# Small-tile mixer products gathered into pinned visits between a decoder trunk's streamed products

## The chip, the core and the metric

The kernel runs on one NeuronCore of a Trainium2 chip. The metric is the device time of one execution in microseconds (us); lower is better. The engines are PE (TensorE: matmul), ACT (ScalarE), DVE (VectorE), POOL (GpSimd) and SP (SyncE, which issues most of the transfers from the chip's memory).

## What is computed

Two layers of a decoder trunk for one prompt of 256 tokens and 8 samples of 4 tokens, 288 columns in all, in 32-bit floats.

```
u = RMSNorm(x)                                  1024 wide
cols = u @ W_in                                 four mixers and four gates
o_A = conv4 -> RG-LRU, times GeLU gate          256 wide
o_B = RWKV-7 delta-rule state, 4 heads of 64
o_C = HGRN2, 4 heads, state 128 x 64
o_D = dilated sliding-window attention, 4 heads of 64, over cached keys for the samples
x += W_o( sum_n sigmoid(G_n) * (o_n @ P_n) )
x += W_down( gelu(causal_dwconv3(v @ W_gate)) * (v @ W_up) ),   v = RMSNorm(x)
then a last RMSNorm
```

The outputs are the trunk's result and every mixer's new states.

## The kernel before

Activations lie with features on the 128 partitions and the 288 tokens along the columns. A weight chunk of 128 x 1024 comes by one transfer into a buffer `w`, is split by ACT into a rounded half `h` and by DVE into the remainder `l` (`chunk`, three buffers each), and gives 24 products of 128 x 128 weights with 288 columns: for each of eight input blocks high x high, high x low and low x high (`prod`). These are the **streamed** products, 3600 in a layer: 30 chunks of projection (`proj`, numbered by `PROJ`), four gates of eight chunks (`gates`), each followed by the branch product with `in_wb`, then the output projection and the feed-forward part.

`ORDER = "pA pB pC g0 g2 pD g1 g3"` is the order of the streamed work up to the output projection: the projections of mixer A (4 chunks), B (8) and C (12), gate 0 with the branch product of A, gate 2 with that of C, the projections of D (6), gate 1 with that of B, gate 3 with that of D. In chunks of 24 products that is 4 + 8 + 12 + 10 + 10 + 6 + 10 + 10 = 70; this stretch is called the mixing stage here. A branch product cannot start before its mixer has put its result into `ys`.

The mixers are Python generators (`branch_a`, `branch_b`, two of `branch_c`, `branch_d`) that run while the program is traced. `unit` emits nine or six streamed products and then calls `mix`, which lets up to four mixers go on to their next `yield`; `GAP` sets how many calls a mixer of a kind then sits out. B starts a second generator for its samples (kind S, `samples` in `branch_b`), D one for the attention over the cached keys (kind E, `samples` in `branch_d`). So the tracing gives an order in the program text. From it the framework's scheduler makes each engine's final order with its own model of times, by readiness and by place in the text; it hands out tile buffers in that order too. PE, like the other engines, then runs its list as it stands.

The mixers' products are of two sorts. Some use the whole array (in the profile 128*128, or 96*128): transposes `tr`, group sums `exact` over the constant `blk`, and state products. Others use a smaller array tile: 64*128, 128*64, 64*64, 64*32, 128*32, 32*64 or 32*32 rows and columns, several of them side by side. `quads` of B, a recursive inverse, makes 32*32 products; `level_out` of C makes 64-column blocks for seven levels of a decay tree, at the first three with a further small product for the samples; `scores` of B and D makes 64*128 ones. PSUM has eight banks: `pm` 3 for streamed results, `xb` 2 for B, S and E, `xc` 3 for A, C, D and the norms. The tag `b` has 20 buffers, for B and, later, for the feed-forward's activations (`hparts`).

C ends with a product over `zs` that gives the samples' output, a state update, then squares, a sum over `blk` (tiles `a`), logarithm, exponential, three multiply steps and a split into `y`. E loads 16 blocks of keys (`in_kc`, `load_k`) and 16 of values (`in_vc`, `load_v`), four at a time, into the tag `c2` of ten buffers.

Of the kernel before, what the change touches and what calls it, by code (L numbers as in the profile page):

```python
# [127 lines left out]
def dkeys():  # L128
# [7 lines left out]
        "tmp": (1152, 4), "rs": (1152, 1), "a": (1280, 10), "b": (1152, 20), "kb": (2048, 10), "c2": (2688, 10), "kc": (2048, 7),  # L136
# [3 lines left out]
GAP = {"B": 2, "S": 0, "C": 1, "D": 1, "E": 3}  # L140
STEPS = 4
# [9 lines left out]
def trunk(ctx, tc, I, O):  # L151
# [25 lines left out]

    def mm(o, a, b, start=True, stop=True):
        return nc.tensor.matmul(o, a, b, start=start, stop=stop)  # L179
# [269 lines left out]
    def branch_a(l, cols, rs, ys):  # L449
# [26 lines left out]
        for i in range(2):  # L476
# [3 lines left out]
            for j in range(1, 4):  # L480
                stt(xc, e[:, j:j + w], pcol(l, "acw", 2 * j + i), xc, MUL, ADD)
            pg, pa = X("xc")[:, :w], X("xc")[:, :w]
            mm(pg, gw[:, i], xc)
            mm(pa, gw[:, 2 + i], xc)
            yield
# [35 lines left out]
    def branch_b(l, cols, rs, ys_, spawn):  # L521
# [25 lines left out]
        at, rt, bt, kt, bv, elast = [], [], [], [], [], []  # L547
# [3 lines left out]
        pre = []  # L551
        for i in range(2):
            f = slice(i * P, (i + 1) * P)

            pw, pa = X("xb")[:, :N], X("xb")[:, :N]
            first = mm(pw, lora[0:64, 0, f], wa[0:64])
            with tc.issue_after(first.ins):
                mm(pa, lora[64:128, 0, f], wa[64:128])

            kk = T("b")  # L560
            act(kk, k[i], AF.Square, scale=pcol(l, "kk", i))
            yield
            lw, ta = T("b"), T("b")
# [7 lines left out]
        for i in range(2):  # L571
            pn = X("xb")[:, :N]
            exact(pn, bones, pre[i][3], "b")
            yield
            ts(pre[i][3], pn, 1e-24, MAX, float(2 ** 20), MUL)
# [4 lines left out]
        for i in range(2):  # L580
# [6 lines left out]
            b = T("b")  # L587
            stt(b, ta, 1.0, kk, ADD, MUL)

            ep, em = T("b"), T("b")  # L590
# [26 lines left out]
            stt(rk, rk, pcol(l, "rk", i), k2, MUL, MUL)  # L617
            pb = X("xb")[:, :N]
            exact(pb, bones, rk, "b")
            yield  # L620
# [5 lines left out]
        def samples():  # L626
# [4 lines left out]
            p = X("xb")  # L631
# [5 lines left out]
            yield  # L637
# [11 lines left out]
            p = X("xb")  # L649
            for h in range(4):  # L650
                i, z = h // 2, 64 * (h % 2)
                one = ident[rows(h), rows(h)]
                mm(p[z:z + NS, i * 64:i * 64 + 64], bt[i][rows(h), sc], one)
                mm(p[z + NS:z + 64, i * 64:i * 64 + 64], kt[i][rows(h), sc], one)
            act(stk[:, :P], p[:, :P], AF.Copy)
            uv = R([P, 2, 64], "sm")
            for h in range(4):
                z = 64 * (h % 2) + NS
                G.tensor_copy(uv[z:z + NS, h // 2], vh[hr(h)])
            p = X("xb")  # L660
            for h in range(4):
                mm(p[hr(h), :NS], abT[hr(h)], Xi[hr(h)])
            yield
            act(t1, p[:, :NS], AF.Copy)
            p = X("xb")
            for h in range(4):
                mm(p[hr(h), :NS], t1[hr(h)], Y[hr(h)])
            yield
# [7 lines left out]
            for src in (at, rt):  # L676
                p = X("xb")
                for h in range(4):
                    mm(p[hr(h)], src[h // 2][rows(h), sc], s0[h // 2][rows(h)].rearrange("p b v -> p (b v)"))
                yield  # L680
# [3 lines left out]
                sar.append(t)  # L684
            p = X("xb")
            for h in range(4):
                mm(p[hr(h), :64], zs[hr(h), 0], vh[hr(h)])
            yield
            rr, u = T("sm", 64), T("sm", 64)
            tt(V, rr, p[:, :64], sar[0], ADD)  # L690

            p = X("xb")
            for h in range(4):
                mm(p[hr(h), :64], Y[hr(h)], rr[hr(h)])
            yield
            act(u, p[:, :64], AF.Copy)
            for h in range(4):
                z = 64 * (h % 2)
                G.tensor_copy(uv[z:z + NS, h // 2], u[hr(h)])
            for i in range(2):  # L700
                p = X("xb")
# [5 lines left out]
            yield  # L707

            for i in range(2):
                ue = R([P, NB, 64], "kb")  # L710
                tt(G, ue, bc(uv[:, i], 1, [P, NB, 64]), bc(C("vexp"), 2, [P, NB, 64]), MUL)
                p = X("xb")
                for z in range(2):
                    mm(p[rows(z)], stk[rows(z), i * 64:i * 64 + 64], ue[rows(z)].rearrange("p b v -> p (b v)"))
                yield
# [9 lines left out]
        def scores(a, q):  # L725

            ps_ = [X("xb"), X("xb")]
# [6 lines left out]
        ab, abo = (R([P, 8, 64], "kb") for _ in range(2))  # L734
        sab = scores(bt, at)
        yield
# [12 lines left out]
        for pair in (((0, bt, 0), (0, kt, 1)), ((0, v, 2), (1, v, 2)), ((1, bt, 0), (1, kt, 1))):  # L749
            p = X("xb")  # L750
            for n, (i, src, _) in enumerate(pair):
                for c in range(2):
                    tr(p[:, (2 * n + c) * P:(2 * n + c + 1) * P], src[i][:, c * P:(c + 1) * P])
            yield
            for n, (i, _, m) in enumerate(pair):
                tk[i][m] = T("b", 256)
                act(tk[i][m], p[:, n * TP:(n + 1) * TP], AF.Copy)
# [8 lines left out]
        def quads(a, b, to=(0, 1, 2, 3), src=(0, 1, 2, 3)):  # L766

            p = X("xb")
# [5 lines left out]
        for m in (2, 4, 8, 16):  # L774
            p = quads(ab[:, :, 0:32], X4)
            yield
            t1 = R([P, 8, 32], "kb")
            act(t1, p, AF.Copy)
            p = quads(Y4, t1)
            yield  # L780
            V.copy_predicated(X4, Mn(f"l{m}", 8), p)
            V.transpose(fl(Y4), fl(X4))

        Y, Xi = R([P, 8, 64], "kb"), R([P, 8, 64], "kb")
        G.memset(Y, 0.0)
        G.memset(Xi[0:64], 0.0)
        p = quads(ab[:, :, 32:64], X4, (1, 3), (0, 2))
        yield
# [8 lines left out]
        p, p2 = quads(t1, Y4, (0, 2), (1, 3)), quads(Y4, t1, (1,), (1,))  # L797
        yield
# [3 lines left out]

        p = blocks(abo, Xi, (0,), 1)
        yield
        t1, Z = R([P, 8, 64], "kb"), R([P, 8, 64], "kb")
        act(t1[64:128], p[64:128], AF.Copy)
        G.tensor_copy(Z[64:128], Y[64:128])
        p = blocks(t1, Y, (1,), 0)
        yield
# [3 lines left out]
        zz = [[], []]  # L813
        for a, q, mk in ((kt, at, "us"), (bt, rt, "ui"), (kt, rt, "ui")):
            pair = scores(a, q)
            yield
            for h, p in enumerate(pair):
                z = R([P, 4, P], "kb")
                G.memset(z, 0.0)
                V.copy_predicated(z, Mn(mk, 4), p)  # L820
                zz[h].append(z)
        def hc(h):
            return slice(64 * h, 64 * h + 64)
        st = None
        for c in range(2):
            s = slice(c * P, c * P + P)
            p = X("xb")
# [7 lines left out]
            yield  # L835
            rr = T("b", 256)
            act(rr, p[:, :256], AF.Copy)
            p = X("xb")
# [5 lines left out]
            yield  # L844
            u = R([P, 2, P], "b")
            act(fl(u), p[:, :256], AF.Copy)
            p = X("xb")
# [5 lines left out]
            yield  # L853
# [15 lines left out]
            p = X("xb")  # L869
            for i in range(2):  # L870
                if c:
                    mm(p[:, i * P:(i + 1) * P], st[:, i], rt[i][:, s], start=True, stop=False)
                for m in (2, 1):
                    for h in range(2):
                        o, tc_ = p[rows(h), i * P:(i + 1) * P], slice(c * P + 64 * h, c * P + 64 * h + 64)
                        mm(o, tk[i][2][:, tc_] if m == 2 else u[:, i, hc(h)], zz[h][m][:, 2 * i + c],
                           start=c == 0 and m == 2, stop=m == 1)
            yield
            for i in range(2):
                act(py[i][:, s], p[:, i * P:(i + 1) * P], AF.Copy)  # L880
# [5 lines left out]
        for i in range(2):  # L886
            p = X("xb")[:, :N]
            exact(p, cent, py[i], "b")
            yield
# [4 lines left out]
        for i in range(2):  # L894
            p = X("xb")[:, :N]
            exact(p, bones, sqs[i], "b")
            yield
# [3 lines left out]
        for i in range(2):  # L901
            sq, yc = sqs[i], py[i]
            stt(yc, yc, pcol(l, "lnw", i), sq, MUL, MUL)
            stt(yc, yc, pcol(l, "lnb", i), bv[i], ADD, ADD)
# [698 lines left out]
```

## Time and profile before

| | |
|---|---|
| median of three runs | 1210.65 us (1209.11 to 1214.6) |
| profiled execution, its own time | 1212.02 us |
| its span, first to last instruction | 1210.2 us |
| PE, DVE, ACT, POOL busy | 97%, 70%, 51%, 46% of the span |
| PE instructions | 10564 matmuls |
| mean transfer rate | 162 GB/s |
| mixing stages with small products | 54 to 346 us and 649 to 939 us |

Busy time of PE is the union of its instructions' spans, and a matmul's end is modelled; a busy PE can still run at less than its best rate. What a product costs is read from the starts of neighbouring ones. In a timeline row the first number is the start, the second how long the group took, and x the count of products in it.

### The profile page before, as it was taken

Reading aid. Unit: us, or ns where it says so; the run is one execution under the profiler, and the core shown is the slowest. Engines: PE = TensorE matmul, PEld = TensorE weight load, DVE = VectorE, ACT = ScalarE, POOL = GpSimd, SP = SyncE. Lnnn points to the kernel's source line nnn. Section 1 sums busy time; section 2 is a strip of 40 time slices with the busy share of each in tenths; the row PEclk is TensorE's granted clock in tenths of the full one; section 3 lists DMA queues with packets and bytes.
Section 4 is the critical chain, followed back from the end, with each engine's and each line's share of the span. In section 5 each row is a group of like instructions: output and inputs, shape, how many; then the busy total and the mean of one; then the engine's idle time right before and its main releaser. Section 6 shows DMA issues by size and latency. Waiting matters only on the chain.

```text
span 1210.2 us, 26415 instructions
## 1 busy us (share of the span) xinstructions
PE 1172.3 (97%) x10564; PEld 1102.2 (91%) x10564; DVE 848.4 (70%) x1385; ACT 611.3 (51%) x1042; POOL 552.8 (46%) x864
## 2 busy tenths in 40 slices
PE   7998999999999999999998999999999999999997
PEld 6987788998999999999998977899889999999996
DVE  7898856566578888865568888566655878888543
ACT  5776447445355444443367844565444554444332
POOL 3744555250345665642238337524221736665322
PEclk9999999999999999999998999999999999999999
DMA  7444145357645555454543432643775445545552
GB/s 258 132 130 141 63 152 203 112 168 277 209 133 190 161 171 168 164 176 163 171 153 124 141 106 89 214 145 115 253 250 168 150 152 171 172 158 171 167 171 77
DMA packets 64043, 196.33 MB, mean 162 GB/s; under 512 B 8417, under 2 KB 12641, under 8 KB 63921
## 3 DMA queue, kind: packets, MB, share of 16 engines
q1 hardware_dynamic: 61872, 189.56, 47.4%
q0 software_dynamic: 1328, 4.33, 1.0%
q8 instruction: 83, 1.36, 0.5%
q10 hardware_dynamic: 720, 0.76, 0.2%
q14 instruction: 40, 0.32, 0.1%
HBM read 187.08 MB, written 6.49 MB: 160 GB/s over the span
## 4 chain that ended last, share of the span: by engine, by line
PE 74%; DVE 9%; POOL 6%; ACT 4%; DMA 4%; issue 3%; DVEq 0%; SPq 0%; ACTq 0%; POOLq 0%
PE pm L179 43%; PE xc L179 24%; PE xb L179 5%; DVE c L193 2%; DVE l L193 2%; POOL b L193 1%; ACT L185 1%; DMA c<-in_vc 1%; DMA w<-in_w 1%; DVE b L196 1%; POOL a L193 1%; ACT a L185 1%; ACT h L185 1%; PE xc L182 1%; DMA kc<-in_cs 1%
## 5 line engine op out<-in xcount | busy, mean ns | idle before, releaser
L179 PE MATMUL pm<-tp,h 128*128 128x288 f32 x2880 | 608.3, 302 | 3.8 <-ACT h L185 2.3
L185 ACT ACTIVATE h<-w 128x1024 fp32r<-128x1024 f32 x299 | 316.5, 1059 | 393.8 <-issue 182.1
L179 PEld LDWEIGHTS pm<-tp,h 128*128 128x128 f32 x2880 | 471.3, 191 | 17.7 <-issue 7.3
L193 DVE TENSOR_TENSOR l<-w,h 128x1024 fp32r<-128x1024 f32 x299 | 380.6, 1273 | 118.6 <-ACT h L185 117.6
L179 PE MATMUL pm<-tp,l 128*128 128x288 f32 x1440 | 430.4, 299 | 4.5 <-DVE l L193 4.5
L179 PEld LDWEIGHTS pm<-tp,l 128*128 128x128 f32 x1440 | 274.7, 191 | 7.1 <-DVE l L193 5.0
L179 PE MATMUL xc<-tp,h 128*128 128x288 f32 x896 | 183.9, 296 | 1.6 <-ACT tp L185 0.9
L179 PEld LDWEIGHTS xc<-tp,h 128*128 128x128 f32 x896 | 144.7, 188 | 3.3 <-ACT tp L185 1.3
L179 PE MATMUL xc<-tp,l 128*128 128x288 f32 x448 | 132.3, 295 | 0.0
L193 POOL TENSOR_TENSOR tmp<-a,rs 128x256 f32<-128x256 f32 x96 | 73.5, 785 | 71.7 <-ACT a L185 71.7
L193 POOL TENSOR_TENSOR tp<-tp,th 128x288 f32<-128x288 f32 x48 | 52.3, 1111 | 109.3 <-DVE th L196 109.3
L196 DVE SCALAR_TENSOR_TENSOR a<-a,pv,a 128x304 f32<-128x304 f32 (+2 forms) x112 | 83.8, 749 | 11.2 <-ACT a L185 9.5
L179 PEld LDWEIGHTS xc<-tp,l 128*128 128x128 f32 x448 | 84.3, 188 | 0.4 <-DVE l L193 0.4
L193 POOL TENSOR_TENSOR tmp<-x 128x288 f32<-128x288 f32 x28 | 28.2, 1008 | 108.2 <-DVE x L193 107.9
L193 DVE TENSOR_TENSOR th<-pm,rs 128x288 f32<-128x288 f32 x64 | 29.1, 455 | 59.3 <-PE pm L179 59.2
L193 POOL TENSOR_TENSOR c<-c 128x512 f32<-128x512 f32 (+2 forms) x32 | 36.9, 1173 | 35.4 <-DVE kb L193 25.4
L193 DVE TENSOR_TENSOR tmp<-pm,tmp 128x288 f32<-128x288 f32 x48 | 22.0, 458 | 40.1 <-POOL tmp L193 40.1
L185 ACT ACT_TABLE_LOAD x34 | 43.6, 1283 | 0.6
L185 ACT ACTIVATE c<-c 128x256 f32<-128x256 f32 (+2 forms) x68 | 30.6, 500 | 20.9 <-POOL c L193 15.5
L185 ACT ACTIVATE a<-a 128x304 f32<-128x304 f32 (+2 forms) x76 | 33.6, 445 | 13.6 <-DVE a L196 7.8
L193 DVE TENSOR_TENSOR c<-c,c 128x256 f32<-128x256 f32 (+2 forms) x56 | 38.8, 734 | 1.7 <-ACT c L185 1.4
L179 PE MATMUL pm<-y,h 128*128 128x288 f32 x192 | 39.8, 299 | 0.0
(302 smaller groups left out, 1879.1 us busy)
## 6 DMA issues: line engine op xcount, KB each, us to landing
w<-in_wf SPq DMA_DIRECT2D x96, 512.0 KB, 3.5
w<-in_wg SPq DMA_DIRECT2D x64, 512.0 KB, 3.8
w<-in_w SPq DMA_DIRECT2D x59, 512.0 KB, 3.6
w<-in_wd SPq DMA_DIRECT2D x48, 512.0 KB, 3.5
c<-in_kc SPq DMA_DIRECT2D x32, 320.0 KB, 6.2
c<-in_vc SPq DMA_DIRECT2D x32, 320.0 KB, 5.3
w<-in_wb SPq DMA_DIRECT2D x16, 512.0 KB, 3.6
w<-in_wo SPq DMA_DIRECT2D x16, 512.0 KB, 3.5
```

Of the source, the lines that this page charges most:

```text
L179: return nc.tensor.matmul(o, a, b, start=start, stop=stop)
L182: nc.tensor.transpose(o, i, ident)
L185: S.activation(o, i, f, **kw)
L193: e.tensor_tensor(o, a, b, op)
L196: V.scalar_tensor_tensor(o, a, s, b, op0, op1)
```

## The change

- Every product is traced in a kind: streamed (`s`), of a visit (`v`), or a full-array product of a mixer (`f`). With `behind`, an ordering edge on PE, each product of a visit is tied behind the one before it, the first behind the last streamed product traced, and the next streamed product behind the visit's last. The `f` products are not tied, nor are the other streamed ones to each other.
- `mix` now runs the steps of kind `f` at each call, but those of kind `v` only once 22 or more streamed products have gone by since the last visit. As calls come after 9, 9 and 6 products, that is after 24. A step's own wait is counted in streamed products too: 9 after an `f` step, 18 before the next `v` step, and 30, 36 or 48 where the text says so. `STEPS` and `GAP` are gone.
- Where a mixer must wait for something before the streamed work can go on, `mix(True)` lets time run on without streamed products.
- Yields now stand ahead of the products instead of behind them, and steps are joined: both first-stage products of B in one step; the samples' second product of S with the first; each C level with its sample product, levels 4 and 8 as one step, 16 and 32 as one; in B's scores, `kt` against `at` and `rt` side by side in one tile `ar` (8 products of 256 columns for 16 of 128); in B's chunks, state and output products in one step; in E, key blocks 0 and 1, 2 and 3, value blocks 0 and 1, 2 and 3.
- Some small products become full-array ones: transposes of 32 columns now take 128, and C's sample transposes go with the others. B's token-major transposes become a generator of their own.
- `b` goes from 20 to 16 buffers, a new tag `ar` has two of 2304 bytes, `exact` in B takes its two halves from `yb`.

```diff
-GAP = {"B": 2, "S": 0, "C": 1, "D": 1, "E": 3}
-STEPS = 4
+VISIT = 22
...
+    kind, now, last = ["s"], [0], {"s": None, "v": None, "open": False}
+
+    def behind(ins, prev):
+        tc.add_manual_dep(ins.ins, prev.ins.name, mybir.DependencyInfo(
+            mybir.DependencyClass.NoSync, mybir.DependencyReason.DATA), reason="order on PE")
+
     def mm(o, a, b, start=True, stop=True):
-        return nc.tensor.matmul(o, a, b, start=start, stop=stop)
+        ins = nc.tensor.matmul(o, a, b, start=start, stop=stop)
+        if kind[0] == "v":
+            behind(ins, last["v"] if last["open"] else last["s"])
+            last["v"], last["open"] = ins, True
+        elif kind[0] == "s":
+            if last["open"]:
+                behind(ins, last["v"])
+                last["open"] = False
+            last["s"] = ins
+            now[0] += 1
+        return ins
...
+        for i in range(2):
+            yield "v"
+            pair = [X("xb"), X("xc")]
+            for c in range(2):
+                s = slice(c * P, c * P + P)
+                for h in range(2):
+                    mm(pair[h][:, c * TP:(c + 1) * TP], kt[i][rows(h), s], ar[i][rows(h), :, s])
...
+            level = (d, d, f"u{m}", f"s{m}" if m <= 2 else None)
+            if m in (4, 16):
+                first = level
+                continue
+            yield "v", 30
+            level_out(*([level] if m <= 2 else [first, level]))
...
                 for g in range(4):
                     mm(s1[quarter(g), 0:P], qb[:, j, 2 * g + n // 2], ks[g][:, 512:640], start=f, stop=z)
-                yield
                 if n < 2:
                     load_k(n + 2)
+                if n == 1:
+                    yield "v", 48
...
+        def steps(which):
+            for x in list(mixers):
+                if x[1] > now[0] or (x[2] == "v") != (which == "v"):
+                    continue
+                kind[0] = which
+                try:
+                    state = next(x[0])
+                except StopIteration:
+                    mixers.remove(x)
+                    continue
+                finally:
+                    kind[0] = "s"
+                gap = 0
+                if state != "wait":
+                    state, gap = state if isinstance(state, tuple) else (state, 0)
+                    gap = max(gap, 18 if state == "v" else 9)
+                x[1], x[2] = now[0] + gap, state
+
+        def mix(idle=False):
+            steps("f")
+            if idle or now[0] - visited[0] >= VISIT:
+                visited[0] = now[0]
+                steps("v")
+            if idle:
+                now[0] += 9
...
             while n not in ys:
-                mix()
+                mix(True)
```

## Rows read from the trace of the kernel before

**Rows 1.** Windows: us, busy us (count) of PE, PEld, DVE, ACT, POOL; clock; DMA share, GB/s.
```profile
54.00:346.00 292.00, 282.26 (x3031) 250.58 (x3031) 198.88 (x353) 157.07 (x318) 121.52 (x176) 0.98 0.48 161
390.00:480.00 90.00, 90.00 (x683) 90.00 (x682) 74.87 (x117) 41.47 (x59) 57.87 (x109) 1.00 0.53 169
649.00:939.00 290.00, 280.70 (x3024) 249.01 (x3022) 198.34 (x350) 155.30 (x317) 118.16 (x170) 0.98 0.49 162
100.00:155.00 55.00, 49.79 (x667) 40.39 (x666) 47.91 (x90) 25.16 (x59) 29.93 (x36) 0.97 0.25 83
```

**Rows 2.** Timeline of PE, first and last small-tile group of the first layer.
```profile
55.85 0.76 PE L179 MATMUL xb<-b,kb 64*128 64x288 f32 x4
...
319.09 1.30 PE L179 MATMUL xb<-c,c 128*32 128x128 f32 x40
```

**Rows 3.** Timeline of PE around one small-tile group of E.
```profile
309.55 0.42 PE L179 MATMUL pm<-yb,h 128*128 128x288 f32 x2
309.81 0.29 PE L179 MATMUL pm<-yb,l 128*128 128x288 f32 x1
310.03 1.30 PE L179 MATMUL xb<-c,c 128*32 128x128 f32 x40
311.26 0.53 PE L179 MATMUL pm<-yb,h 128*128 128x288 f32 x2
311.63 0.29 PE L179 MATMUL pm<-yb,l 128*128 128x288 f32 x1
```

**Rows 4.** Timeline of PE, a narrow window: the last four of those forty.
```profile
311.04 0.29 PE L179 MATMUL xb<-c,c 128*32 128x128 f32 x4
```

**Rows 5.** Timeline of PE, narrow windows: one small tile straight after another.
```profile
119.37 0.63 PE L179 MATMUL xb<-kb,b 64*32 64x512 f32 x4
...
119.82 0.61 PE L179 MATMUL xb<-kb,b 64*32 64x512 f32 x4
...
120.36 0.45 PE L179 MATMUL xc<-c,c 128*64 128x64 f32 x8
```

**Rows 6.** Waits of PE: total us, times, longest.
```profile
PE xb L179 <- ACT b L185: 6.2, 2, 3.4
...
PE pm L179 <- DVE l L193: 4.5, 3, 2.1
PE xc L179 <- DVE c L193: 4.1, 6, 1.1
```

**Rows 7.** Windows of the lowered clock in the mixing stages, first and last.
```profile
70.03:73.44 3.41, 3.41 (x16) 3.41 (x16) 3.41 (x7) 3.39 (x8) 1.61 (x3) 0.50 0.07 26
...
704.91:708.32 3.41, 3.41 (x17) 3.41 (x15) 3.41 (x9) 0.29 (x1) 2.39 (x4) 0.50 0.45 150
```

**Rows 8.** Timelines of PE, ACT and POOL: C's end and the product that needs it.
```profile
201.09 0.67 PE L179 MATMUL xc<-a,blk 128*128 128x288 f32 x3
...
201.92 0.50 ACT L185 ACTIVATE a<-xc,few 128x288 f32<-128x288 f32 x1
202.44 1.28 ACT L185 ACT_TABLE_LOAD   x1
...
211.21 0.80 POOL L193 TENSOR_TENSOR y<-a,y 128x288 fp32r<-128x288 f32 x1 [4.43 <-ACT y L185]
213.17 1.61 POOL L193 TENSOR_TENSOR y<-a,y 128x288 fp32r<-128x288 f32 x1 [1.17 <-ACT y L185]
...
231.36 0.54 PE L179 MATMUL pm<-y,h 128*128 128x288 f32 x2
```

**Rows 9.** Timeline of PE at the mixing stage's end.
```profile
346.86 0.40 PE L179 MATMUL xc<-tp,h 128*128 128x288 f32 x1 [0.45 <-ACT tp L185]
347.10 0.43 PE L179 MATMUL pm<-y,h 128*128 128x288 f32 x2
```

**Rows 10.** Transfers by line: count, KB each, median us to landing.
```profile
c<-in_kc SPq DMA_DIRECT2D x32, 320.0 KB, 6.2
```

**Rows 11.** Windows, columns as in rows 1: the stretch of E's key loads.
```profile
270.00:300.00 30.00, 30.00 (x239) 23.48 (x232) 18.71 (x41) 14.99 (x36) 1.98 (x5) 1.00 0.80 283
```

More of the change, by code (lines that the diff above doesn't have):

```diff
@@ L550, in branch_b @@
         els = R([P, 2, NB], "sm")
-        pre = []
+        pre, pwa = [], []
+        yield "v"
         for i in range(2):
             f = slice(i * P, (i + 1) * P)
[L555 to L558, printed above, removed]
+            pwa.append((X("xb")[:, :N], X("xc")[:, :N]))
+            for z, p in enumerate(pwa[i]):
+                mm(p, lora[rows(z), 0, f], wa[rows(z)])
+        for i in range(2):
+            pw, pa = pwa[i]
             kk = T("b")
             act(kk, k[i], AF.Square, scale=pcol(l, "kk", i))
-            yield
-            lw, ta = T("b"), T("b")
+            ar.append(R([P, 2, N], "ar"))
+            lw, ta = ar[i][:, 0], T("b")
             act(lw, pw, AF.Tanh, scale=0.5, bias=dcol(l, "hw0", i))
@@ L636, in samples @@
                 mm(p[hr(h), P:P + 64], v[h // 2][rows(h), sc], ident[rows(h), rows(h)])
-            yield
+            for h in range(4):
+                i, z = h // 2, 64 * (h % 2)
+                one = ident[rows(h), rows(h)]
+                mm(p2[z:z + NS, i * 64:i * 64 + 64], bt[i][rows(h), sc], one)
+                mm(p2[z + NS:z + 64, i * 64:i * 64 + 64], kt[i][rows(h), sc], one)
             abT, Y, Xi, t1 = (T("sm", NS) for _ in range(4))
@@ L648, in samples @@
             act(vh, p[:, P:192], AF.Copy)
[L649 to L655, printed above, removed]
+            act(stk[:, :P], p2[:, :P], AF.Copy)
             uv = R([P, 2, 64], "sm")
@@ L843, in branch_b @@
                     mm(p[64:128, o], Z[:, z], rr[:, o])
-            yield
             u = R([P, 2, P], "b")
             act(fl(u), p[:, :256], AF.Copy)
-            p = X("xb")
+            yield "v"
+            p, po = X("xb"), X("xc")
+            if c:
+                for i in range(2):
+                    mm(po[:, i * P:(i + 1) * P], st[:, i], rt[i][:, s], start=i == 0, stop=False)
             for i in range(2):
@@ L852, in branch_b @@
                         mm(o, tk[i][m][:, tc_], tk[i][2][:, tc_] if m else u[:, i, hc(h)], start=m == 1, stop=m == 0)
-            yield
+            for i in range(2):
+                for m in (2, 1):
+                    for h in range(2):
+                        o, tc_ = po[rows(h), i * P:(i + 1) * P], slice(c * P + 64 * h, c * P + 64 * h + 64)
+                        mm(o, tk[i][2][:, tc_] if m == 2 else u[:, i, hc(h)], zz[h][m][:, 2 * i + c],
+                           start=c == 0 and m == 2, stop=m == 1 and c <= i)
             if c == 0:
@@ L868, in branch_b @@
                 nc.sync.dma_start(O["b_wkv_p"][l], nst)
-            p = X("xb")
             for i in range(2):
[L871 to L880, printed above, removed]
+                act(py[i][:, s], po[:, i * P:(i + 1) * P], AF.Copy)
             st = nst
@@ L1400, in gates @@
             while n not in ys:
-                mix()
+                mix(True)
             y = ys[n]
@@ L1432, in trunk @@
         while mixers:
-            mix()
+            mix(True)
         mg = []
```

260 lines of the change are left out of this document (132 added, 128 removed).

## The prediction

> **What bounds the kernel now.** I read the windows first. In the feed-forward stretch PE is busy all the time and starts 683 products in 90 us [rows 1]: 0.132 us for a streamed product, and PE is the limit. The two mixing stages take 292 and 290 us with the clock at 0.98 and PE busy 96 to 97% [rows 1]. Of their 70 chunks of 24 products about 53 fall into these windows, so streamed work explains 53 x 24 x 0.132 = 168 us; some 123 us in each layer go to mixer products, to changing between array tiles, and to waits. That is where the change acts. In the part from 100 to 155 us DVE is busy 47.9 of 55 us [rows 1], so there it is nearly as full as PE.
>
> Next, the timeline of PE, for what a change of array tile costs. Between streamed products the start moves on 0.13 us at a time (309.55 for two, 309.81). The first small product starts at 310.03, 0.22 after the last streamed one: 0.09 late [rows 3]. The forty run four abreast; from 310.03 to the last four at 311.04 is nine steps of 0.112 us; the first streamed product follows after 0.22, at 311.26, so 0.11 late [rows 3, 4]. The next pair takes 0.37 to 311.63 where 0.26 is usual: 0.11 more [rows 3]. One small-tile group between streamed products, a *visit*, thus costs 0.31 us beside its own work. Straight from one small tile to another: four products of 64*32 take 0.45, the next four 0.54 until the 128*64 ones start [rows 5]: 0.09.
>
> I counted the groups in the timeline from the first to the last of the first layer [rows 2]: 65 visits, and 33 direct changes inside them; the second layer has the same numbers.
>
> Third, the waits of PE: 6.2 us on ACT's `b`, 4.5 on `l`, 4.1 on C's `c` [rows 6], over both layers. After longer waits the granted clock is 0.50, the 1.2 GHz level, for 3.41 us or more; there are five such stretches in the mixing stages [rows 7].
>
> **The switches (term 1).** I walked through the yields with the rule of the new `mix`. B has 21 `v` steps, S 10, each C 9, D 3, E 4. Steps of different mixers that fall due together share a visit. In the first layer the first visit comes after chunk 14 (B's first products), S and B run side by side to chunk 26, B and the two Cs to chunk 42, and D and E use five visits from chunk 54 to 63: 32 visits with 18 direct changes, as B's 32*32 groups stand beside C's 128*64. In the second layer the counter starts at another phase, both Cs fall into the same visits, and it is 29 visits and 13 changes. Saved: (33 + 36) x 0.31 + (15 + 20) x 0.09 = 21.4 + 3.2 = 24.6; I take -24. The lower bound is half of it, -12: only the first streamed product after a visit is tied behind it, so the scheduler could let others, or `f` products, into a visit that its model finds not ready.
>
> The Trainium skill, TensorEngine Tiling (Array Packing), Key Properties, says that going to another tiling mode drains the array, while going to another tile of the same mode does not; it gives no price. With one price for every change of mode, 0.31 / 2 = 0.155, an estimate, 163 changes a layer would fall to 82 and 71, and the saving would be 27. The rows make the direct change cheaper than half a visit, and I go by them.
>
> The work of the products themselves stays: 8 products of 256 columns stream as many columns as 16 of 128. I cost that at nothing. The added DVE work, four more masked copies in B's scores and two or three short ones in each C, is hidden while PE sets the pace. If DVE does (it is at 87% from 100 to 155), it costs about 3 us a layer; S, B and C now stretch over 28 chunks, where that stretch of the trace has 55 us of them at once, so I expect cover. Fewer `b` buffers: by my count at most 15 live at once in B, since `lw` and `ep` moved to `ar` and the halves to `yb`. Nothing for that.
>
> **Gate 2 waits for C (term 2).** The same walk puts C's last small product at chunk 41.75 in the first layer and 40.75 in the second, and gate 2's branch product wants C's result at chunk 42. Before, the result was there at 214.8 (213.17 + 1.61) and was first used at 231.36: 16.6 us to spare [rows 8]. That reserve is gone. From C's sum to its finished result it took 201.09 to 214.8, 13.7 us; a copy, a square and a split stand ahead, about 1.6 at 0.4 each (ACT's step of this size from PSUM takes 0.50 [rows 8]). So at most 15.3. At least: two table loads of 1.28, nine short steps at 0.5 and POOL's 0.80 [rows 8], 7.9. Less the streamed work left (0.25 and 1.25 chunks of 3.2 us), PE would stand 7 to 14.5 us in one layer and 4 to 11.3 in the other, 18.6 at the middles. But a later streamed product can pass a waiting one: at 346.86 one of the output projection stands among the branch products [rows 9]. Here D's projections could pass, one chunk at a time, since two of three weight buffers are held by the waiting branch product. I let them fill half: +9, between 0 and +26.
>
> **E's transfers (term 3).** Key blocks 2 and 3 are requested when the first key visit gives buffers back, and their visit is due 48 streamed products later: 6.3 us, 7.6 with the second half of the first visit. Eight transfers of 320 KB [rows 10] are 2.6 MB, and the busiest stretch moved 283 GB/s with the transfer engines at 0.80 [rows 11]: 9.3 us, 1.7 late. The same holds for the values, so four times in the run. SP's queue has the weight chunks too; those have slack in three raw and three split buffers. I take 1.2 each, +5, between 0 and 3 each (+12).
>
> **The waits (term 4).** 7.5 us of the waits stand before small products (the 4.1 on `c` and the longest of 3.4 on ACT's `b`). A `v` step now comes at least 24 streamed products, 3.2 us, after the one it follows, so I take half away: -4. The rest, 2.8 us before a sum over `blk` and 4.5 before streamed products on `l`, is not touched by the ties. What the lowered clock costs I leave: waits that go take theirs along, and the one at gate 2 brings its own. Bounds: -23 (14.8 us of waits and half of five stretches of 3.41 gone), and on the other side the rival below.
>
> **Sum.** 1212.0 (the profiled execution: span 1210.2 and 1.8 around it; the median of the runs, 1210.65, is 1.4 lower) - 24 + 9 + 5 - 4 = **1198 us**.
>
> **Rivals.** *The visits block PE (slower).* A visit stands at a fixed place; if its first operand is late, PE stands, and with it every streamed product behind, then DVE and ACT, which wait for their results, then the `w` buffers and SP. For it speaks DVE at 87% in C's stretch, where each level takes two multiplies of DVE after POOL and ACT; against it that the spacing is generous. There are 61 visits: a mean wait of 0.33 us takes 20 us and turns the forecast slower than before; at 0.45 us it is 1198 + 27 = 1225. The Trainium skill, TensorE: Matmul & The Clock Gate, Part 3, The mechanism, says that matmuls begin and end strictly in order and only weight loads are pulled ahead; by that rule nothing behind a late visit could run, and it ends as this rival. The trace agrees so far: the waits of PE are idle time with streamed work queued behind [rows 6].
>
> *The gain is eaten up (no change).* Nothing passes at gate 2 (+18.6) and E is 1.7 late: 1212 - 24 + 18.6 + 6.8 - 4 = 1209. The other way there is that the change doesn't do what it says: with visits broken up, the saving is 12, and 1198 + 12 = 1210.
>
> *All goes well (faster by more).* Waits and lowered clock vanish (-23) and gate 2 fills with D's chunks: 1212 - 24 - 23 + 5 = 1170, or about 1178 with half of term 2.
>
> **How the numbers follow.** Forecast, 1184 to 1204: 0.40. All well, below 1184: 0.15. No change, 1205 to 1217 (a difference under 0.5%, 6 us, is about what a measurement of this kernel can't tell from none): 0.20. Blocked visits, above: 0.25. So 0.55 faster, 0.20 the same, 0.25 slower. The range from 1178 to 1224 leaves out about half of the blocked case and half of the best one. The forecast's own range is 1184 to 1204.
>
> **What would show it.** Term 1: some 30 small-tile groups a layer in place of 65, 24 streamed products apart. Term 2: a gap on PE between the last gate 2 product and the first branch product on `y`, near chunk 42, waiting for POOL or ACT `y`, with D's projections in it if they pass. Term 3: waits of PE's `xb` products on `in_kc` and `in_vc`. Term 4 and the first rival: PE's waits on DVE `c`, ACT `b` and `kb` in the list of waits, smaller or larger than now, and the number of stretches at 0.50. Wrong would be, above all, waits of over 20 us before small products, or visits split up.

## The result, and the profile after

The changed kernel takes 1249.7 us (median of four runs, 1248.61 to 1253.22) beside 1210.12 us for the kernel before on the same chip: a ratio of 1.0325, interval 1.0292 to 1.0358. The forecast was 1198 us, range 1178 to 1224: wrong in sign, with 0.25 on slower. The profiled execution took 1249.95 us (before: 1212.02), and the difference of 37.9 us lies in the mixing stages, which take 38.2 longer in the account below.

First the windows of the first layer, columns as in [rows 1]: C's projections; gate 0 with its branch product; gate 2's streamed work; what then passes before the branch product on `y` starts. First before (the last two parts are one there, as there is no pause), then after.

```profile
54.00:106.80 52.80, 48.85 (x378) 44.83 (x378) 47.07 (x86) 43.37 (x91) 28.36 (x41) 0.97 0.41 131
106.80:187.90 81.10, 76.55 (x1283) 62.64 (x1284) 60.07 (x111) 36.50 (x91) 44.64 (x64) 0.98 0.40 131
187.90:231.40 43.50, 42.50 (x370) 40.07 (x368) 22.95 (x35) 25.27 (x42) 12.72 (x18) 0.96 0.44 152
```
```profile
54.30:128.90 74.60, 60.61 (x833) 52.40 (x833) 59.30 (x116) 48.14 (x101) 36.10 (x54) 0.91 0.33 101
128.90:181.90 53.00, 53.00 (x715) 48.02 (x714) 36.17 (x77) 22.40 (x45) 18.58 (x28) 1.00 0.36 116
181.90:231.20 49.30, 47.90 (x484) 43.01 (x483) 27.61 (x45) 30.72 (x73) 21.19 (x38) 1.00 0.47 157
231.20:252.20 21.00, 5.35 (x11) 2.45 (x9) 12.81 (x23) 18.45 (x32) 4.07 (x6) 0.55 0.50 162
```

Three things stand there. C's projections take 74.6 us for 52.8, and PE has 833 products in them for 378: mixer work has moved forward into this part. Gate 0's part is shorter, 53.0 for 81.1, with 715 products for 1283. And behind gate 2's streamed work comes a pause of 21 us in which PE is busy for 5.35. The streamed work from the end of C's projections to gate 2's branch product now takes 231.2 - 128.9 = 102.3 us, where it took 124.6.

The pause in the timeline of PE; before it, the branch product followed without a gap [rows 8].

```profile
230.03 0.29 PE L186 MATMUL xc<-cst,sm 32*64 32x32 f32 x4
...
234.53 1.33 PE L186 MATMUL xb<-b,kb 128*128 128x288 f32 x2 [3.11 <-ACT b L202]
236.46 0.77 PE L186 MATMUL xc<-kc,a 96*128 96x512 f32 x1 [0.60 <-ACT a L202]
240.57 0.77 PE L186 MATMUL xc<-kc,a 96*128 96x512 f32 x1 [3.34 <-DVE a L210]
...
242.88 0.98 PE L186 MATMUL xc<-a,blk 128*128 128x288 f32 x2
252.23 1.48 PE L186 MATMUL pm<-y,h 128*128 128x288 f32 x4 [8.38 <-ACT y L202]
...
261.06 0.42 PE L186 MATMUL pm<-tp,h 128*128 128x288 f32 x2
```

C's last small products start at 230.03, the last of its state products (96*128) at 242.25, its last sums at 242.88, and `y` is first used at 252.23. D's first projection product comes at 261.06, behind the branch product: nothing passed. Yet D's first weight chunk was split and ready at 239.74 (DVE):

```profile
238.52 1.22 DVE L210 TENSOR_TENSOR l<-w,h 128x1024 fp32r<-128x1024 f32 x1
```

The Trainium skill, TensorE: Matmul & The Clock Gate, Part 3, The mechanism, says that matmuls begin and end strictly in order; the trace agrees, with 8.38 us of idle time before a waiting product and a chunk of ready projections behind it.

The list of PE's waits after (total, times, longest), against [rows 6]:

```profile
PE pm L186 <- ACT y L202: 15.4, 2, 8.4
PE xc L186 <- DVE a L210: 9.5, 5, 3.3
PE pm L186 <- DVE l L210: 7.6, 7, 4.1
PE xb L186 <- ACT yb L202: 6.0, 3, 3.3
...
PE pm L186 <- ACT h L202: 5.1, 5, 2.2
PE xb L186 <- ACT b L202: 4.5, 2, 3.1
PE pm L186 <- DVE a L210: 4.3, 2, 4.1
PE xb L186 <- ACT ar L202: 3.8, 1, 3.8
PE xc L186 <- POOL sm L1045: 2.8, 1, 2.8
...
PE xb L186 <- DMA c<-in_vc: 0.6, 1, 0.6
```

Most stand before full-array products (B's sums on `yb` and `ar`, C's state products on `a`) and before streamed products (`y`, `l`, `h`). Counted in the mixing stages, 6.8 us stand before the small products of a visit, 2.8 of them on `sm`; before, it was 11.4. E's transfers cost 0.6.

The clock is at 0.50, the 1.2 GHz level, for 23.89 us at each pause at gate 2, from 2 us into it to 4 or 5 us past its end; before, the five stretches of the lowered clock in the mixing stages were mostly of the length in [rows 7]. At its end the branch products, 0.24 us apart until then, are 0.13 apart again.

```profile
233.44:257.33 23.89, 10.22 (x29) 7.41 (x30) 11.87 (x24) 16.24 (x29) 7.97 (x11) 0.50 0.37 120
844.42:868.31 23.89, 10.24 (x29) 7.36 (x30) 14.10 (x24) 16.66 (x34) 7.69 (x10) 0.50 0.38 127
```
```profile
253.51 0.44 PE L186 MATMUL pm<-y,l 128*128 128x288 f32 x1
253.75 0.68 PE L186 MATMUL pm<-y,h 128*128 128x288 f32 x2
...
257.75 0.30 PE L186 MATMUL pm<-y,l 128*128 128x288 f32 x1
257.88 0.43 PE L186 MATMUL pm<-y,h 128*128 128x288 f32 x2
```

**The account.** For each kernel I split the mixing stage of both layers, from its thirteenth chunk on, in three: *waits* (idle time of PE over 0.06 us before a product), *clock* (half of the time at 0.50 outside these waits, an estimate by the 0.24 and 0.13 us above), and *rest* (what is left: the products and the array changes at full clock). Visits are counted as in [rows 2], both layers.

| kernel | stage | rest | waits | clock | visits |
|---|---|---|---|---|---|
| before | 590.9 | 561.0 | 19.8 | 10.0 | 130 |
| after | 629.1 | 538.7 | 66.3 | 24.1 | 78 |
| change | +38.2 | -22.3 | +46.5 | +14.1 | -52 |

So rest fell by about what was forecast for the array changes, and waits and clock took back almost three times as much.

**B and C have changed places.** C's first level, in the timelines of before (two rows) and after:

```profile
107.24 0.34 PE L179 MATMUL xc<-c,c 128*64 128x64 f32 x4
...
114.62 0.45 PE L179 MATMUL xc<-c,c 128*64 128x64 f32 x6
```
```profile
144.82 0.80 PE L186 MATMUL xc<-c,c 128*64 128x64 f32 x18
```

and the first 32*32 step of B's inverse, again before and after:

```profile
138.47 0.72 PE L179 MATMUL xb<-b,kb 32*32 32x32 f32 x61
```
```profile
98.40 0.75 PE L186 MATMUL xb<-b,kb 32*32 32x32 f32 x64
```

B's inverse starts 40 us earlier, C's levels 38 us later. C's result is wanted at gate 2, B's only at gate 1, some 70 us later. C's operands were there long before; DVE after (its last step of `k`, and the factors of the next levels):

```profile
115.90 2.85 DVE L219 TENSOR_SCALAR c<-c,der 128x256 f32<-128x256 f32 x4
...
124.35 0.81 DVE L210 TENSOR_TENSOR c<-c,c 128x288 f32<-128x288 f32 x2
```

From C's first level to its last sum it takes about the same time as before (98 us for 95): it is not slower, it starts later. (The spacing of the visits sets this time too: it is 72 us in x10 below.)

Two things used up the reserve at gate 2. Before, C's first level came 0.4 us after the end of C's projections, with 2 streamed products between them in the timeline of PE; after, 15.9 us, with 79 between: 15.5 us. And the streamed work from the end of C's projections to gate 2's branch product became 22.3 us shorter. Together that is 37.8 us, about the old reserve of 16.6 and the new pause of 21.0. The other 22 of the 38 us by which C starts later are C's longer projections. Since C's operands were ready, the 79 products are C's place in PE's list, not a wait; whether the counts in `mix` or the ties put it there is not shown (without ties there are 66 and 157 of them in the two layers of x1, 2 and 81 in x17).

### The profile page after: what moved, and what is told of

Its sections match the earlier page's. It is cut to its first block, busy times and chain, and to the rows that moved or that the text cites. A ratio compares the mean times of both kernels' runs of the same rounds, so it can differ in the third digit from the quotient of the medians.

```text
span 1248.2 us, 26286 instructions
## 1 busy us (share of the span) xinstructions
PE 1165.0 (93%) x10496; PEld 1098.7 (88%) x10496; DVE 848.9 (68%) x1409; ACT 625.0 (50%) x1054; POOL 540.4 (43%) x864
## 5 line engine op out<-in xcount | busy, mean ns | idle before, releaser
L186 PEld LDWEIGHTS pm<-tp,l 128*128 128x128 f32 x1440 | 276.1, 192 | 11.4 <-DVE l L210 9.7
L186 PE MATMUL pm<-y,h 128*128 128x288 f32 x192 | 43.3, 320 | 15.4 <-ACT y L202 15.4
L210 POOL TENSOR_TENSOR c<-c 128x512 f32<-128x512 f32 (+2 forms) x32 | 33.8, 1075 | 43.5 <-PE xc L186 31.2
L186 PEld LDWEIGHTS pm<-y,h 128*128 128x128 f32 x192 | 33.4, 205 | 17.1 <-ACT y L202 16.3
L202 ACT ACTIVATE a<-a 128x304 f32<-128x304 f32 (+3 forms) x76 | 33.4, 445 | 13.4 <-DVE a L213 9.6
```

The lines of the kernel that those rows point to most:

```text
L186: ins = nc.tensor.matmul(o, a, b, start=start, stop=stop)
L202: S.activation(o, i, f, **kw)
L210: e.tensor_tensor(o, a, b, op)
```

## The experiments

Ratios are to the kernel before, on the same chip.

**First: ties, pace, place of C.** The theory at this point: the pace of the steps brings C after gate 2. Rivals: the ties (R1), fewer buffers (R2).

`x1_no_ties`:
```diff
     def behind(ins, prev):
-        tc.add_manual_dep(ins.ins, prev.ins.name, mybir.DependencyInfo(
-            mybir.DependencyClass.NoSync, mybir.DependencyReason.DATA), reason="order on PE")
+        return
```


> The changed kernel without its ordering edges (behind does nothing); the steps, their pace and the joins stay. Theory (the pace brings C's result after gate 2, and waits at gate 2 and before B's whole-array sums make the time): the two waits at gate 2, some 20 us each, stay; 1235 to 1255 us. Rival R1 (the ties make PE wait): most of the 46 us of new waits go, 1190 to 1212 us.

Measured 1243.71 us, 1.0287 (1.0269 to 1.0304), which overlaps with the changed kernel's interval. Waits 54.1, clock 14.7, rest 551.7, 89 visits: without ties the visits break up (48 direct changes for 26), rest is 13 us higher, and 12 us of waits and 9 of clock go. By the prices of the prediction the counted changes are only some 5 of the 13. The waits at gate 2 stay (14.2 and 16.5). R1 falls as the main cause.

`x2_c_pace`:
```diff
-            yield "v", 30
+            yield "v"
             level_out(*([level] if m <= 2 else [first, level]))
```


> The changed kernel with C's levels 18 streamed products apart instead of 30. Theory: C's result comes some 3 chunks of 3.2 us earlier, the wait at gate 2 falls from 21 to about 10 us a layer and part of the lowered clock with it: 1215 to 1230 us. Rival R1 (ties) or R2 (fewer buffers in B) alone: the visits come closer together, waits no smaller: 1245 us or more.

Measured 1246.37 us, 1.0311 (1.0296 to 1.0326): outside what the theory gave, and the time is that of its rivals, though the waits did shrink. The waits in gate 2's part fell from 17 to 6 and from 18 to 9, clock rose to 30.9, and 8 us of waits came up elsewhere; at gate 2 there now stand B's last sums, which the same loop puts ahead of the branch product. The quicker pace alone does not help.

`x3_c_first`:
```diff
-ORDER = "pA pB pC g0 g2 pD g1 g3"
+ORDER = "pA pC pB g0 g2 pD g1 g3"
```


> The changed kernel with the projections of C ahead of those of B (ORDER pA pC pB g0 g2 pD g1 g3); ties, pace and joins stay. Theory: C ends about 7 chunks before gate 2 asks for it, so the waits at gate 2 and their lowered clock (about 2 x 21 us, and 2 x 6 for the clock) go: 1195 to 1212 us, unless B's sums wait more. Rival R1 (ties) or R2 (buffers): the waits stay wherever the visits stand, 1240 us or more.

Measured 1236.02 us, 1.0226 (1.0211 to 1.0242). The waits at gate 2 are gone, 0 and 2.2:
```profile
192.50:233.90 41.40, 41.40 (x622) 37.34 (x620) 23.84 (x38) 27.38 (x54) 22.81 (x35) 0.96 0.50 169
```
but gate 0's part now waits 12.6 and 11.6 us where the changed kernel had none (45.7 us of waits in all). The gain is 14 us where 38 or more were looked for.

`x4_before_c_late`:
```diff
-GAP = {"B": 2, "S": 0, "C": 1, "D": 1, "E": 3}
+GAP = {"B": 2, "S": 0, "C": 3, "D": 1, "E": 3}
```


> The kernel before with GAP of C 3 instead of 1, so that C's steps come half as often, without ties, joins or any other part of the change. Theory: C comes after gate 2 here too, with a wait of 10 us or more a layer and the clock at 0.50 behind it: 1230 us or more. Rival R1 or R2: no ties and all buffers are here, so 1205 to 1215 us.

Measured 1267.00 us, 1.0491 (1.0464 to 1.0517). In the kernel before, with no part of the change, C's lateness alone brings the same picture, last sum and branch product:
```profile
252.54 0.61 PE L179 MATMUL xc<-a,blk 128*128 128x288 f32 x1 [0.43 <-DVE a L193]
262.08 1.48 PE L179 MATMUL pm<-y,h 128*128 128x288 f32 x4 [8.94 <-ACT y L185]
```
Waits 57.1 and clock 16.1: like the changed kernel. Rest is 571.7, 11 more than before, with 156 visits; that part is not the lateness.

**Second: more room at gate 2, later sums.**

`x5_g2_after_pD` (the changed kernel) and `x6_before_g2_after_pD` (the kernel before):
```diff
-ORDER = "pA pB pC g0 g2 pD g1 g3"
+ORDER = "pA pB pC g0 pD g2 g1 g3"
```


> The changed kernel with gate 2 after the projections of D (ORDER pA pB pC g0 pD g2 g1 g3), so that C's result is wanted 6 chunks, 19 us, later. Theory (what failed is the reserve at gate 2): the waits ahead of gate 2's branch product (17 and 18 us) and the lowered clock around them (24 us a layer at half speed) go, the waits in C's projections (14 and 16 us) stay: about 1250 - 35 - 17 = 1198, so 1195 to 1215 us. Rival (DVE and ACT simply have no more to give in the stretch of S, B and C, and a wait moved is a wait found elsewhere): 1235 us or more.

> The control: the kernel before with the same order (gate 2 after D's projections). It had 16 us to spare at gate 2 already, so by the theory nothing is won: 1203 to 1215 us. If it gets as much faster as the changed kernel does, the order is good by itself and says nothing of the ties and the pace.

Measured 1254.77 us, 1.0355 (1.0334 to 1.0375), and 1240.97 us, 1.0250 (1.0222 to 1.0279). Both misses: more room at gate 2 wins nothing, as the rival of x5 had it. In the changed kernel the wait stands in D's projections instead (PE, then POOL):
```profile
238.43 0.85 PE L186 MATMUL pm<-tp,h 128*128 128x288 f32 x2 [7.76 <-DVE a L210]
```
```profile
229.58 1.12 POOL L1180 DMA_DIRECT2D a<-in_rope  x2
234.32 0.93 POOL L210 TENSOR_TENSOR a<-a,rs 128x288 f32<-128x288 f32 x1 [3.62 <-DMA a<-in_rope]
```
D's first columns are multiplied with tables that are loaded into tiles `a` at 229.58, just as C's last tiles `a` are read (its sums end at 230). So it looks as if D waits for C here too; that C holds these buffers is read from the times, not tried. Why the kernel before loses 30 us by this order (rest +16.7, waits +9.6, 140 visits) I did not settle.

`x7_b_sums_later`, and `x8_both` (this and the order of x5):
```diff
         for i in range(2):
-            yield
+            yield None, 30
             pn = X("xb")[:, :N]
             exact(pn, bones, pre[i][3], "yb")
```


> The changed kernel with B's two sums over blk (ahead of S) each 30 streamed products behind the step ahead of them, in place of 9. Theory (the untied whole-array steps come too close behind the steps that feed them): the waits of 3 to 4 us at 65 us and of 3.3 and 1.2 at 675 us go, some 8 to 10 us in all, but B and S end 1.5 chunks later and the wait at gate 2 does not shrink: 1240 to 1252 us. Rival R2 (the halves in yb, four buffers, hold the sums up): the waits stay where they are, 1248 us or more.

> Both edits: gate 2 after D's projections, and B's sums 30 products behind. Theory: the gains add, 1188 to 1208 us, which would be faster than the kernel before. Rival (DVE and ACT have no more to give): 1235 us or more.

Measured 1247.54 us, 1.0301 (1.0283 to 1.0318), and 1246.67 us, 1.0295 (1.0274 to 1.0315). In x7 the first wait before a sum falls from 3.77 to 2.02, and others grow; waits 65.0 for 66.3. As the theory of that moment said, but it tells nothing: C's projections still wait 14.5 and 15.1 us. For x8 the theory was wrong by 39 us or more.

**Third: the mixing loop, the density, and C's pace once more.**

`x9_old_pace` runs the new steps in the loop of before (`GAP`, at most four steps a call) without ties; `x11_old_pace_ties` does so with them:
```diff
-            if idle or now[0] - visited[0] >= VISIT:
-                visited[0] = now[0]
-                steps("v")
+            for x in list(mixers):
+                if x[1] > slot[0]:
+                    continue
```


> The changed kernel with its new steps, joins, buffers and whole-array products, but with the mixing loop of before (up to four steps at each call, GAP 2, 2, 0, 1, 1, 3, no ties, no visits every 24 products). Theory, second form (the rule that paces the steps costs the time, not the steps themselves): the waits of PE in the mixing stages fall from 66 us to 20 to 30, and the joins alone save part of the 22 us of array changes: 1195 to 1215 us. Rival R2 (the steps: fewer buffers, the sums' halves in yb, the products now ahead of their yields): the waits stay above 45 us, 1235 us or more.

> As x9 (the mixing loop of before, with the new steps), but each small-tile product tied in its place between the streamed ones. Theory (pace, not ties): within 12 us of x9. Rival R1 (ties): 20 us or more above x9.

Measured 1269.36 us, 1.0482 (1.0448 to 1.0515), and 1293.27 us, 1.0673 (1.0643 to 1.0703). So the second form of the theory (the pace rule alone) fell: under the old loop the new steps are slower still, with waits of 64.9 us, as the rival R2 (the steps and their fewer buffers) had it. R2 was not tried by itself. In x9 C's first level comes at 164.95, 44 us after C's projections, although it has a step at each call and no tie, and gate 2 waits 10.16 at once:
```profile
164.95 0.68 PE L186 MATMUL xc<-c,c 128*64 128x64 f32 x14
```
```profile
258.95 1.54 PE L186 MATMUL pm<-y,h 128*128 128x288 f32 x4 [10.16 <-ACT y L202]
```
Ties cost 24 us there, as R1 had it. What this pair suggested was where to look: not how fast C goes but when it starts, and who runs first.

`x10_dense`:
```diff
-VISIT = 22
+VISIT = 14
...
-                    gap = max(gap, 18 if state == "v" else 9)
+                    gap = max(gap, 9)
...
-            yield "v", 30
+            yield "v"
```


> The changed kernel with visits some 15 to 18 streamed products apart in place of 24, v steps 9 apart in place of 18 and C's levels unspaced; ties stay. Second theory (pace): C's waits at gate 2 go down by half or more, the array changes rise by some 5 to 8 us: 1225 to 1240 us. Rival (ties: a fixed place costs the wait whatever the spacing): stalls at least as large, 1250 us or more.

Measured 1240.70 us, 1.0243 (1.0214 to 1.0273). The time is just above the expected range. Gate 2 hardly waits (0.4 and 3.1), but C's projections wait 22 and 24 us, mostly for B:
```profile
PE xb L186 <- ACT yb L202: 13.1, 6, 4.7
PE xb L186 <- DVE yb L210: 7.0, 6, 2.5
PE xb L186 <- DVE b L803: 6.3, 2, 4.4
PE xb L186 <- DVE b L213: 6.0, 2, 3.9
```

`x12_before_c_2` is x4 with 2 in place of 3.

> The kernel before with GAP of C 2 instead of 1, between the kernel before (1210) and the one with 3 (1267 beside 1209). Second theory (C's pace alone sets the wait at gate 2): part of that cost, 1215 to 1245 us, with waits at gate 2 between 1 and 21 us a layer. Rival: no difference to before, 1205 to 1215 us, if only the widest spacing uses up the reserve.

Measured 1252.96 us, 1.0345 (1.0318 to 1.0372). That is above the expected range; gate 2's part waits 14.4 and 13.4 us, as expected. With `GAP` of C at 1, 2 and 3 the kernel before takes 1210, 1253 and 1267 us. One step of `GAP` uses up its reserve at gate 2, 16.6 us in the first layer [rows 8].

**Fourth: who runs first.**

`x13_b_later_c_pace`; `x14_b_later` has the first two edits, not the third:
```diff
             sc = slice(TP, N)
-            yield "v"
+            yield "v", 96
             p, p2 = X("xb"), X("xc")
...
-        yield "v", 30
+        yield "v", 192
         sab = scores(bt, at)
...
-            yield "v", 30
+            yield "v"
             level_out(*([level] if m <= 2 else [first, level]))
```


> The changed kernel with S 96 and B's scores 192 streamed products later, and C's levels 18 apart in place of 30; ties and joins stay. Third theory (B and C have changed places: B's 32*32 steps start 40 us earlier than before, into C's projections, where PE then waits for DVE and ACT, and C's levels start 38 us later, so that C's chain ends after the streamed work of gate 2): C's first level at about 115 us after the layer's start instead of 139, waits in C's projections from 14 and 16 to about 5 us, at gate 2 from 17 and 18 to 5 or less: 1195 to 1218 us. Rival R1 (ties) or the rival that DVE has no more to give: 1235 us or more.

> As x13, but C's levels stay 30 apart. Third theory: the waits in C's projections go as in x13; C starts earlier but keeps its pace, so some 5 to 10 us a layer of wait at gate 2 may stay: 1205 to 1230 us. If the pace of C alone mattered, it would be 1240 us or more.

`x15_xb_only`, and so for B's and S's other pairs:
```diff
-            ps_ = [X("xb"), X("xc")]
+            ps_ = [X("xb"), X("xb")]
```


> The changed kernel with B's second bank of a pair taken from xb, as before, in place of xc (the first-stage products and no others still use xc). Rival R3 (B's and S's use of xc, of which C has three, keeps C from starting): C's first level within 5 us of the end of C's projections, the wait at gate 2 below 8 us a layer: 1225 us or less. Third theory (the steps' times, not the banks): 1242 to 1256 us.

Measured 1212.35 us, 1.0010 (0.9995 to 1.0024); 1240.07 us, 1.0244 (1.0210 to 1.0278); and 1256.04 us, 1.0366 (1.0338 to 1.0394). The banks (R3) are not it. Holding S and B back, with C's levels closer, takes away the whole loss; holding them back alone takes a quarter away, and x2 had shown that C's pace alone takes almost nothing. They work together. Of the waits, 31 us go at gate 2 and 7 in C's projections, and 7 come back in gate 0's part. Windows of x13, the same three parts as above:

```profile
54.70:117.60 62.90, 51.81 (x402) 46.95 (x402) 53.86 (x107) 45.35 (x89) 31.78 (x51) 0.89 0.31 99
117.60:183.00 65.40, 62.35 (x1181) 55.43 (x1180) 47.72 (x90) 32.56 (x76) 31.13 (x51) 0.97 0.33 107
183.00:232.30 49.30, 46.38 (x396) 40.19 (x395) 30.09 (x49) 30.64 (x64) 19.57 (x28) 1.00 0.59 198
```
C's projections have 402 products again, near the 378 of before. C's first level and last sum, and the branch product:
```profile
131.17 0.51 PE L186 MATMUL xc<-c,c 128*64 128x64 f32 x10
```
```profile
220.00 0.43 PE L186 MATMUL xc<-a,blk 128*128 128x288 f32 x2
```
```profile
232.29 0.78 PE L186 MATMUL pm<-y,h 128*128 128x288 f32 x4
```
14 us earlier at the start and 23 at the end, C is in time: no wait stands before the last row. C's first level is at 125 us where 115 was expected, though, still 68 streamed products after C's projections, and these wait 11 us a layer where 5 was expected. Waits are still 36.9 and clock 20.5, against 19.8 and 10.0 before; that eats the 27.5 us by which rest is lower (533.5).

`x16_b_later_still` is x13 with 192 and 264 in place of 96 and 192, and the sums of x7; `x17_b_later_no_ties` is x13 without ties; `x18_sums_too` is x13 with the sums of x7 alone.

> As x13 (1212), with B's two first sums 30 products behind the step ahead of them, S another 96 and B's scores another 72 products later, so that nothing of S and no 32*32 step of B is left in C's projections; B's result had 40 us to spare at gate 1 in x13. Third theory: the 11 us of waits a layer in C's projections fall to 5 and part of the lowered clock goes: 1190 to 1206 us, faster than both kernels. Rival (DVE has no more to give; the waits come back beside C's levels or at gate 1): 1210 us or more.

> x13 without the ordering edges. In the changed kernel they were worth 6 us against (1243.7 without, 1249.7 with). If the ties still cost more waiting than the array changes they save: 1202 to 1209 us. If, with B and C in their places, the ties are what saves: 1214 us or more.

> x13 (1212) with B's two first sums 30 products behind the step ahead of them, and S and B's scores as in x13. In x16, which moved S and the scores too, the waits in C's projections fell from 11 to 7.5 us a layer, but 4 to 5 us came back at gate 2 and more beside C's levels. If the sums were what helped in x16: 1202 to 1210 us, faster than both kernels. If it was S and the scores: 1210 to 1216 us.

Measured 1224.03 us, 1.0108 (1.0090 to 1.0127); 1227.65 us, 1.0134 (1.0112 to 1.0155); 1223.84 us, 1.0107 (1.0085 to 1.0130). In x16 the waits in C's projections fall from 11 to 7.5 a layer, and 4.1 and 4.8 us come back before the branch product on `y`, more beside C's levels: the rival of that run holds. x18 is worse than x13 too, outside both of its ranges, with more waits in the same parts. No version was faster than the kernel before. x17 turns x1 round: in x13 the ties are worth 15 us (rest 554.2 without, 533.5 with). The counted array changes explain some 5 of these 20.7 us by the prices of the prediction; most of the others lie between the small products of one tile, whose starts are on average 36 ns apart without ties and 30 with them, for a reason that no run shows.

| kernel | stage | rest | waits | clock | C's first level | C's last sum | gate 2's branch | B's inverse from |
|---|---|---|---|---|---|---|---|---|
| before | 590.9 | 561.0 | 19.8 | 10.0 | 101 | 196 | 225 | 132 |
| after | 629.1 | 538.7 | 66.3 | 24.1 | 139 | 237 | 246 | 92 |
| x2 | 624.0 | 539.1 | 54.0 | 30.9 | 140 | 229 | 244 | 93 |
| x3 | 614.3 | 544.9 | 45.7 | 23.6 | 83 | 197 | 226 | 161 |
| x10 | 619.6 | 531.9 | 60.2 | 27.6 | 160 | 232 | 243 | 92 |
| x12 | 630.8 | 569.7 | 42.5 | 18.7 | 101 | 231 | 247 | 132 |
| x13 | 590.8 | 533.5 | 36.9 | 20.5 | 125 | 214 | 226 | 117 |
| x14 | 616.7 | 546.0 | 51.8 | 18.9 | 125 | 228 | 237 | 117 |
| x16 | 602.9 | 535.3 | 43.9 | 23.8 | 117 | 210 | 221 | 132 |
| x17 | 604.4 | 554.2 | 34.2 | 16.1 | 105 | 218 | 230 | 121 |

The first columns are worked out as above; the last four are us from the first streamed product of the first layer. Rest holds more than array changes: x10, with 79 visits, has 6.8 us less of it than the changed kernel with 78.

## Why the prediction was wrong

**Term 1 was right.** Forecast -24; rest fell by 22.3. I had 61 visits; there were 78, and the direct changes inside them fell from 66 to 26, so 52 x 0.31 + 40 x 0.09 = 19.7. That the time came within 2 us is partly luck, by what else lies in rest.

**Term 2 is the step that failed.** It has +9 with a bound of 26. Waits in gate 2's part rose from 1.0 and 1.0 to 17.1 and 18.1, so by 33, past the bound already, and the lowered clock comes on top. The place was right: counted in streamed products, C's last small product stands at chunk 41.75 of the first layer, as forecast, and at 41.54 of the second, where 40.75 was forecast. Two things were wrong. First, the tail from that product was taken as 7.9 to 15.3 us, from the sum on; between them stand four whole-array steps of C's state update and B's last products, and it took 252.23 - 230.03 = 22.2, and 23.0 in the second layer. Second, half of the pause was to be filled by D's projections, and none passed. [rows 9] show the order of PE's list there; the branch product behind has no wait, so nothing overtook a waiting product. With the measured tails and nothing passing, the same sum gives pauses of 21.4 and 21.5 us; the traces have 21.0 and 22.1. (The middles of the forecast's own ranges add up to 18.4, not 18.6.)

**The places of B and C were not looked at.** I counted the visits in which S and B run beside C, and even noted their start at chunk 14, but read it only as a count of visits. That B's inverse then starts 40 us earlier, in a part where DVE was at 47.07 of 52.8 us already, stands nowhere in the sum. C's projections took 22 us longer, with waits of 14 and 16 us where 4 and 3.5 had been. Holding S and B back (x13, x14) takes away 11 to 12 of these 22 us a layer, but only 3 to 4 us of the waits, so the early place of S and B is shown for about half of it. x4 and x12 show, in the kernel before, that slowing C alone costs 57 and 43 us, of which 11 and 9 are rest.

**Term 4 had the sign wrong**: -4 forecast, waits outside gate 2's part rose by 13. What it reasoned of small products held: the waits before them fell from 11.4 to 6.8 us. Its other half failed, that the waits before sums and streamed products stay as they are: before whole-array and streamed products outside gate 2's part they rose from 8.4 to 27.2, and they are 25.6 in x13. **Term 3** was too high: +5 forecast, 0.6 measured. **The lowered clock** I left at nothing; it cost 14.

**The rival of blocked visits** had the right side and the wrong mechanism: 6.8 of 66.3 us of waits stand before the small products of a visit, and x1 without ties is still 1.0287. The ties are against by some 6 us in the changed kernel (intervals overlap) and by 24 under the old loop, and for by 15 in x13.

What stays open: what the fewer buffers and B's halves in `yb` cost (R2; x13 has them and still reaches the time of before); what puts C's first level so far behind C's projections; why the new steps under the old loop are slower still (x9), why the order of x6 costs the kernel before 30 us, and what holds the 11 us of waits a layer that stay in C's projections in x13; moving the sums or S and B further did not remove them without others.

## What to carry to other kernels

A saving on the busiest engine is only worth what the dependent chains beside it can follow: before taking array changes out of a stretch, compare the length of the chain that must end by its end with the time the stretch will then take. Follow that chain to its last consumer, step by step; here the four whole-array steps between the last small product and the sum were left out. When a change reorders side work, list for each piece when it starts now and when its result is wanted; here B, wanted some 70 us later, moved ahead of C. A reserve of 16.6 us at one join can be found by slowing one chain in the kernel as it stands, with one number changed (x4, x12), before the change is built.

## What the runs showed of the hardware

At each pause at gate 2 the granted clock stayed at 0.50, the 1.2 GHz level, for 23.89 us, in which PE was busy for 10.2. The last 4 to 5 us of it are streamed work behind the pause, 0.24 us a product for 0.13, so a pause costs beyond its own length. Over both layers the lowered clock outside waits cost 24 us by the estimate of the account, 14 more than before, and in x2 it took back 6.8 of the 12.3 us that shorter waits had given.
